# The mLSTM heads' normalisation: column sums on TensorE and a small inverse root, or squares added first, two products of ones, and an inverse root over whole rows

## The chip, the cores and the metric

The kernel runs on one core of a Trainium2 chip. The metric is the device time of one execution in microseconds (us). The kernel before took 1197.71 us, the median of three runs (1197.57 to 1198.04).

The engines are named as in the profile: PE is TensorE's matmul, PEld its weight load, DVE is VectorE, ACT is ScalarE, POOL is GpSimd, and SP is SyncE, which issues most of the loads. "L175" is line 175 of the kernel.

## The reference

The reference is a two-layer streaming encoder over 512 positions and a width of 1024. Layer 0 mixes with an mLSTM (4 heads of 192 columns) and an attention to 256 memory tokens, layer 1 with a chunked band attention and the same kind of memory attention; each layer has a gated MLP with a short convolution behind it. The change touches only what stands behind the mLSTM's weighted sums:

```python
h = num / jnp.maximum(jnp.abs(den), jnp.exp(-m_t))[..., None]
...
hm = hm * lax.rsqrt(jnp.mean(hm * hm, axis=-1, keepdims=True) + EPS)
hm = hm.reshape(bsz, seq, A_WIDTH) * a_head_g[a].astype(jnp.float32)
mix_out = (hm * jax.nn.sigmoid(o.astype(jnp.float32))).astype(x.dtype)
```

`num` is a head's weighted sum of values, `den` the same sum of ones, `m_t` a running maximum of the gates. The kernel never divides by the denominator. With z = max(den^2, exp(-2 m_t)), the normalised row is num / sqrt(mean(num^2) + EPS * z), so that one factor for each position is enough: the inverse root of mean(num^2) + EPS * z.

## The kernel before, in words

Everything is held transposed: columns of the model on the 128 partitions, the 512 positions along the free dimension. A product of full precision is three products of split operands (`mm3`, lines 175 to 177: high by high, high by low, low by high); `split` (L136, L137) makes the two halves, the high one as a copy on ScalarE and the low one as a subtraction on VectorE. Weights come by SP in tiles of 128 columns, go through `split`, and are used by `project`.

`gate_rows` computes the rows of the gates (4 partitions, one for each head, by 512 positions): `ar`, `mr` and running sums, with a maximum of `mr` at L1086. Lines 1096 and 1097 transpose `ar` and `mr` in blocks of 128 positions, so that positions come onto the partitions; L1099 takes exp(-2 mr) there as `floor2` (128 x 4 x 4). It runs beside the value columns and the q, k and o tiles of the first head pair, which call it as filler.

`mlstm_head(h)` has three parts. First the weighted scores in four blocks of keys and the products with the values (L1151 to L1191), which give two banks: `nums[0]` has 128 columns of the head, and `nums[1]` has the other 64 on one half of the partitions (`rs`) and, on the other half, the denominator, 64 times the same row, since the value tiles hold ones there. Then the squares (L1195, ScalarE) and the products of the sums with the o gate (L1197, VectorE). Then the normalisation:

- For each block T of 128 positions, two products (L1202, L1203) with the squares as the stationary operand and two columns of constants (`mcf`) as the moving one. They give, with positions on the partitions, the sum of squares and the mean of the 64 squared denominators.
- L1207 to L1210: the maximum with `floor2`, the factor EPS, the mean, and an inverse root by an integer trick and three Newton steps (`rsqrt`, L219 to L228), all on 128 x 4.
- `diagonal` (L230 to L244) splits the 128 x 4 result and puts each half on four diagonals of 128 x 128; `spread` (L246 to L251) multiplies them with ones (L250), so that the factor of each position stands on all partitions, in a `psc` bank.
- L1216 multiplies the gated sums with it, and `split` puts the result into `mixes`, which the output projection (`OutProjection`) reads.

A head is a generator; `yield n` tells `weave` how much filler to put there. In the first three heads the filler is the projections of the q, k and o tiles and the memory queries, in the fourth head the products of the output projection whose inputs are there already. Between heads 1 and 2 and between heads 2 and 3 stands a memory attention. The parts (0, 4, 5) and (1, 4, 5) of the output projection need heads 2 and 3 and come last. Then `OutProjection.finish` starts the next norm; its `logarithms()` (L255) loads the table set of ScalarE that has both logarithm and exponential.

In this part of the kernel a scheduler orders each engine's instructions, by what is ready and by the order of the program; `pin` keeps an instruction behind the one that its engine was given before. Buffers: three PSUM banks `mm`, three `sc`, two `tr`; eight rows `t`, two rows `bias` (the band attention of layer 1 uses them later).

`Norm.finish` (L272 to L289), used by the norms of whole rows, has a form of its own: `split` of the summed squares, two products of ones (L280), logarithm, exponential and square on ScalarE (L282, L284, L285), and two VectorE operations for one Newton step (L287, L289).

Of the kernel before, what the change touches and what calls it, by code (L numbers as in the profile page):

```python
# [9 lines left out]
F32 = mybir.dt.float32  # L10
F32R = mybir.dt.float32r
I32 = mybir.dt.int32
AF = mybir.ActivationFunctionType
ALU = mybir.AluOpType
AX = mybir.AxisListType

P = 128
D = 1024
S = 512
KT = D // P  # L20
TT = S // P
MEM = 256
AW = 768
AH = 4
DH = AW // AH
BH = 12
HD = 64
# [3 lines left out]
EPS = 1e-6  # L31
# [24 lines left out]
def trunk(  # L56
# [30 lines left out]
    def sb(tag, shape, dtype=F32):  # L87
        count[0] += 1
        return pool.tile(shape, dtype, tag=tag, name=f"{tag}{count[0]}", bufs=bufs[tag])

    def ps(tag):
        count[0] += 1
        return psum.tile([P, S], F32, tag=tag, name=f"p{tag}{count[0]}", bufs=pbufs[tag])

    def small(n=4):
        return sb("s", [P, 32])[:, :n]
# [21 lines left out]
            V.tensor_copy(sel[q], ident[q, 32 * s : 32 * s + AH].unsqueeze(2).to_broadcast([AH, AH, P]))  # L118
    eps = cpool.tile([P, 1], F32, name="eps")
    V.memset(eps, EPS)  # L120

    mcf = cpool.tile([P, 3, 2], F32, name="mcf")
    V.memset(mcf, 0.0)
    V.memset(mcf[:, 0, 0:1], 1.0)
    V.memset(mcf[:HD, 1, 0:1], 1.0)
    V.memset(mcf[HD:, 1, 1:2], 1.0 / HD)
    V.memset(mcf[:HD, 2, 1:2], 1.0 / HD)
    V.memset(mcf[HD:, 2, 0:1], 1.0)


    HEADS = (slice(0, HD), slice(HD, P))

# [2 lines left out]
    def split(hi, lo, src, on_act=True, pinned=False):  # L135
        high = A.copy(hi, src) if on_act else V.tensor_copy(hi, src)  # L136
        low = V.tensor_tensor(out=lo, in0=src, in1=f(hi), op=ALU.subtract)  # L137
        if pinned:
            pin(high)
            pin(low)  # L140
# [78 lines left out]
    def rsqrt(y, v):  # L219
        n = v.shape[-1]  # L220
        yi = y.bitcast(I32)
        V.tensor_scalar(yi, v.bitcast(I32), 1, None, op0=ALU.logical_shift_right)
        V.tensor_scalar(yi, yi, -1, 0x5F3759DF, op0=ALU.mult, op1=ALU.add)
        t = small(n)
        for _ in range(3):
            V.tensor_mul(t, y, y)
            V.scalar_tensor_tensor(t, t, -0.5, v, op0=ALU.mult, op1=ALU.mult)
            V.scalar_tensor_tensor(y, t, 1.5, y, op0=ALU.add, op1=ALU.mult)  # L228

    def diagonal(c):  # L230

        cs = [sb("s", [P, 32], F32R)[:, :TT] for _ in range(2)]
        split(*cs, c, on_act=False)
        dgs = []
        for c in cs:
            dg = sb("t", [P, S], F32R)
            V.tensor_tensor(
                out=dg.rearrange("p (a b) -> p a b", a=TT),
                in0=ident.unsqueeze(1).to_broadcast([P, TT, P]),
                in1=f(c).unsqueeze(2).to_broadcast([P, TT, P]),  # L240
                op=ALU.mult,
            )
            dgs.append(dg)
        return dgs  # L244

    def spread(dgs, tag):  # L246

        o = ps(tag)
        for i, dg in enumerate(dgs):
            nc.tensor.matmul(o, onesr, dg, start=i == 0, stop=i == 1)  # L250
        return o  # L251

    def logarithms():

        pin(A.preload_act_table_set("natural_log_exp_and_others"))  # L255
# [762 lines left out]
    e, u, c, r = (cpool.tile([P, TT, AH], F32, name=f"gate{i}") for i in range(4))  # L1018
    tot = cpool.tile([AH, 16], F32, name="tot")
    acol = cpool.tile([P, TT, AH], F32, name="acol")  # L1020
    floor2 = cpool.tile([P, TT, AH], F32, name="floor2")
    RO = [0, 512, 896, 1152, 1280]

    rp = []
# [1 line left out]
    def gate_rows():  # L1026

        V.tensor_copy(ic, gt[:, :, :AH])
        V.scalar_tensor_tensor(e, fg, -1.0, fg, op0=ALU.mult, op1=ALU.min)
        A.activation(e, e, AF.Exp)  # L1030
        V.tensor_scalar(u, e, 1.0, None, op0=ALU.add)
        A.activation(lf, u, AF.Ln)
        V.scalar_tensor_tensor(c, u, -1.0, e, op0=ALU.add, op1=ALU.subtract)
        V.reciprocal(r, u)
        yield
        pin(V.tensor_mul(c, c, r))
        V.tensor_tensor(out=lf, in0=lf, in1=c, op=ALU.subtract)
        V.scalar_tensor_tensor(lf, fg, 0.0, lf, op0=ALU.min, op1=ALU.subtract)
        yield
        yield  # L1040
        lfp, icp = ps("tr"), ps("tr")
        for T in range(TT):
            nc.tensor.transpose(lfp[:AH, T * P : (T + 1) * P], lf[:, T, :], ident)
            nc.tensor.transpose(icp[:AH, T * P : (T + 1) * P], ic[:, T, :], ident)
        yield
        lfr, br, ar, mr = (sb("t", [P, S])[:AH, :] for _ in range(4))
        rr = [sb("t", [P, S]) for _ in range(2)]
        rp.extend(sb("u", [P, S], F32R) for _ in range(2))
        for t in rp:
            G.memset(f(t), 0.0)  # L1050
        pin(V.tensor_copy(lfr, lfp[:AH, :]))
        yield
        for T in range(TT):
            sl = slice(T * P, (T + 1) * P)
            pin(V.tensor_tensor_scan(br[:, sl], ones[:AH, :], lfr[:, sl], 0.0, ALU.mult, ALU.add))
        yield
        pin(V.tensor_tensor(out=ar, in0=icp[:AH, :], in1=br, op=ALU.subtract))
        yield
        carry = 0.0
        for T in range(TT):  # L1060
            sl = slice(T * P, (T + 1) * P)
            pin(V.tensor_tensor_scan(mr[:, sl], ar[:, sl], ar[:, sl], carry, ALU.max, ALU.max))
            if T < TT - 1:
                e_ = (T + 1) * P - 1
                V.tensor_tensor(out=tot[:, T : T + 1], in0=mr[:, e_ : e_ + 1], in1=br[:, e_ : e_ + 1], op=ALU.add)
                carry = tot[:, T : T + 1]
            yield
        for s in range(TT):
            off = None
            for T in range(s, TT):  # L1070
                sl = slice(T * P, (T + 1) * P)
                dst = rr[s // 2][64 * (s % 2) : 64 * (s % 2) + AH, sl]
                if T == s:
                    pin(V.tensor_scalar(dst, mr[:, sl], -1.0, None, op0=ALU.mult))
                else:
                    end = br[:, T * P - 1 : T * P]
                    if off is None:
                        off = end
                    else:
                        k = 4 + 4 * s + T - s  # L1080
                        V.tensor_tensor(out=tot[:, k : k + 1], in0=off, in1=end, op=ALU.add)
                        off = tot[:, k : k + 1]
                    V.tensor_scalar(dst, mr[:, sl], -1.0, off, op0=ALU.mult, op1=ALU.add)
            yield
        pin(V.tensor_tensor(out=mr, in0=mr, in1=br, op=ALU.add))
        V.tensor_scalar(mr, mr, -40.0, None, op0=ALU.max)  # L1086
        yield
        for s in range(TT):
            q, t = 64 * (s % 2), rp[s // 2]
            src, hi = rr[s // 2][q : q + AH, s * P :], t[q : q + AH, s * P :]  # L1090
            pin(V.tensor_copy(hi, src))
            V.tensor_tensor(out=t[q + 32 : q + 32 + AH, s * P :], in0=src, in1=f(hi), op=ALU.subtract)
            yield
        tp = ps("tr")
        for T in range(TT):
            nc.tensor.transpose(tp[:, T * AH : (T + 1) * AH], ar[:, T * P : (T + 1) * P], ident[:AH, :AH])
            nc.tensor.transpose(tp[:, 16 + T * AH : 16 + (T + 1) * AH], mr[:, T * P : (T + 1) * P], ident[:AH, :AH])
        pin(V.tensor_copy(acol, tp[:, :16].rearrange("p (t h) -> p t h", t=TT)))
        A.activation(floor2, tp[:, 16:32].rearrange("p (t h) -> p t h", t=TT), AF.Exp, scale=-2.0)  # L1099

    mixes = [None] * KT

# [41 lines left out]
    def mlstm_head(h):  # L1144
# [48 lines left out]
        for o, j, r in ((nums[0], full, slice(0, P)), (nums[1], sh, rs)):  # L1193
            sq = sb("t", [P, S])
            A.activation(sq, o, AF.Square)  # L1195
            sqs.append(sq)
            V.tensor_tensor(out=og[j][r, :], in0=o[r, :], in1=og[j][r, :], op=ALU.mult)  # L1197
        yield
        st = ps("sc")
        for T in range(TT):  # L1200
            sl = slice(T * P, (T + 1) * P)
            nc.tensor.matmul(st[:, 2 * T : 2 * T + 2], sqs[0][:, sl], mcf[:, 0, :], start=True, stop=False)  # L1202
            nc.tensor.matmul(st[:, 2 * T : 2 * T + 2], sqs[1][:, sl], mcf[:, 1 + odd, :], start=False, stop=True)  # L1203
            yield 0.581
        st = st[:, : 2 * TT].rearrange("p (t c) -> p t c", c=2)
        z, fc = small(), small()
        V.tensor_tensor(out=z, in0=st[:, :, 1], in1=floor2[:, :, h], op=ALU.max)  # L1207
        V.tensor_scalar(z, z, EPS, 1e-35, op0=ALU.mult, op1=ALU.max)
        V.scalar_tensor_tensor(z, st[:, :, 0], 1.0 / DH, z, op0=ALU.mult, op1=ALU.add)
        rsqrt(fc, z)  # L1210
        dg = diagonal(fc)
        yield 2.673
        fb = spread(dg, "sc")
        yield
        for j, r in ((full, slice(0, P)), (sh, rs)):
            V.tensor_tensor(out=og[j][r, :], in0=fb[r, :], in1=og[j][r, :], op=ALU.mult)  # L1216
# [308 lines left out]
```

## Time and profile before

| what | value |
| --- | --- |
| median of three runs | 1197.71 us |
| span of the profiled execution (first to last instruction) | 1197.4 us |
| instructions in it | 18206 |
| mLSTM heads' column sums (L1202, L1203) | from 125.2 to 247 us |
| ACT table loads of L1112, L582, L255, L1157 | 6, 3, 3, 2 |
| one table load | 1283 ns |
| mean granted TensorE clock | 0.999 |

The page gives the profiled execution's span and no other time for it. Busy times are sums over instructions; a busy matmul time overlaps with its neighbours', since matmuls are pipelined, so that distances between starts are the better measure. In a timeline each line has the start, the duration, engine, line, operation, output <- input, shape, the count and, in brackets, the idle time before it with what ended it. A line of the windows view has the stretch, its length, then busy time and count for PE, PEld, DVE, ACT and POOL, the granted clock, the share of the DMA engines and GB/s. A line of a group has count, busy time, mean duration, and the idle time before. A line of waits has who waited for whom, the total, how often, and the longest.

### The profile page before, as it was taken

Reading aid. Unit: us, or ns where it says so; the run is one execution under the profiler, and the core shown is the slowest. Engines: PE = TensorE matmul, PEld = TensorE weight load, DVE = VectorE, ACT = ScalarE, POOL = GpSimd, SP = SyncE. Lnnn points to the kernel's source line nnn. Section 1 sums busy time; section 2 is a strip of 40 time slices with the busy share of each in tenths; the row PEclk is TensorE's granted clock in tenths of the full one; section 3 lists DMA queues with packets and bytes.
Section 4 is the critical chain, followed back from the end, with each engine's and each line's share of the span. In section 5 each row is a group of like instructions: output and inputs, shape, how many; then the busy total and the mean of one; then the engine's idle time right before and its main releaser. Section 6 shows DMA issues by size and latency. Waiting matters only on the chain.

```text
span 1197.4 us, 18206 instructions
## 1 busy us (share of the span) xinstructions
PE 1186.5 (99%) x6735; PEld 1039.1 (87%) x6735; DVE 967.3 (81%) x1772; ACT 718.4 (60%) x1290; POOL 123.3 (10%) x206
## 2 busy tenths in 40 slices
PE   9999999999999999999999999999999999999997
PEld 8988888888889989999888888888889988999986
DVE  6778688878978888888698888997897888888855
ACT  5646577655655555555575667776565655555545
POOL 1200101000021111111021000001001011011100
PEclk9999999999999999999999999999999999999999
DMA  8634111454266666665563223146336466665551
GB/s 283 212 92 123 54 54 57 134 152 133 88 157 162 153 162 155 151 144 129 152 189 120 89 71 99 55 130 201 116 89 150 110 138 141 141 141 136 121 158 71
DMA packets 199131, 155.97 MB, mean 130 GB/s; under 512 B 7976, under 2 KB 179458, under 8 KB 199042
## 3 DMA queue, kind: packets, MB, share of 16 engines
q1 hardware_dynamic: 183906, 119.74, 34.2%
q0 software_dynamic: 14560, 34.02, 13.7%
q8 instruction: 53, 0.87, 0.3%
q10 hardware_dynamic: 576, 1.05, 0.2%
q14 instruction: 36, 0.29, 0.1%
HBM read 126.27 MB, written 32.44 MB: 133 GB/s over the span
## 4 chain that ended last, share of the span: by engine, by line
PE 93%; DMA 2%; ACT 2%; DVE 2%; issue 0%; SPq 0%; ACTq 0%; DVEq 0%
PE pmm L175 15%; PE pmm L176 15%; PE pmm L177 15%; PE ptr L175 6%; PE ptr L177 6%; PE ptr L176 6%; PE pmm L791 6%; PE psc L177 5%; PE psc L175 5%; PE psc L176 5%; PE pmm L790 3%; PE psc L525 2%; DMA wr<-in_mem_w_kv_dram 2%; PE ptr L1352 1%; PE ptr L1373 1%; PE ptr L1374 1%
## 5 line engine op out<-in xcount | busy, mean ns | idle before, releaser
L175 PE MATMUL pmm<-u,wh 128*128 128x512 f32 (+1 forms) x872 | 309.1, 355 | 0.3 <-ACT u L136 0.2
L176 PE MATMUL pmm<-u,wh 128*128 128x512 f32 (+1 forms) x872 | 306.3, 351 | 0.0
L177 PE MATMUL pmm<-u,wl 128*128 128x512 f32 (+1 forms) x872 | 306.3, 352 | 0.0
L137 DVE TENSOR_TENSOR wl<-wr,wh 128x1024 fp32r<-128x1024 f32 (+3 forms) x172 | 199.8, 1163 | 55.1 <-ACT wh L136 53.1
L136 ACT CAST wh<-wr 128x1024 fp32r<-128x1024 f32 (+3 forms) x172 | 172.1, 1002 | 99.8 <-PE pmm L176 45.2
L177 PEld LDWEIGHTS pmm<-u,wl 128*128 128x128 f32 x872 | 164.5, 189 | 20.9
L175 PEld LDWEIGHTS pmm<-u,wh 128*128 128x128 f32 x872 | 164.5, 189 | 18.7 <-ACT u L136 1.1
L176 PEld LDWEIGHTS pmm<-u,wh 128*128 128x128 f32 x872 | 164.7, 189 | 18.3 <-DVE u L137 0.5
L175 PE MATMUL ptr<-u,wh 128*128 128x512 f32 x272 | 106.7, 392 | 0.0
L177 PE MATMUL ptr<-u,wl 128*128 128x512 f32 x272 | 106.1, 390 | 0.0
L176 PE MATMUL ptr<-u,wh 128*128 128x512 f32 x272 | 105.9, 389 | 0.0
L759 POOL DMA_DIRECT2D xspill<-t x64 | 55.5, 867 | 462.5 <-ACT t L758 457.1
L136 ACT CAST u<-pt 128x512 fp32r<-128x512 f32 x102 | 62.8, 618 | 47.2 <-DVE pt L881 47.1
L137 DVE TENSOR_TENSOR u<-pt,u 128x512 fp32r<-128x512 f32 x102 | 69.9, 689 | 11.2 <-ACT u L136 8.5
L175 PE MATMUL psc<-u,wh 128*128 128x256 f32 (+1 forms) x232 | 76.1, 328 | 0.0
L177 PE MATMUL psc<-u,wl 128*128 128x256 f32 (+1 forms) x232 | 75.9, 327 | 0.0
L176 PE MATMUL psc<-u,wh 128*128 128x256 f32 (+1 forms) x232 | 75.9, 327 | 0.0
L791 PE MATMUL pmm<-u,u 128*128 128x512 f32 x192 | 69.6, 397 | 0.0
L943 ACT ACTIVATE t<-t 128x512 f32<-128x512 f32 x34 | 21.5, 632 | 79.4 <-DVE t L666 79.4
L827 DVE TENSOR_TENSOR t<-t,pmm 128x256 f32<-128x256 f32 x72 | 30.2, 420 | 45.0 <-ACT t L825 45.0
L758 ACT COPY t<-ptr 128x512 f32<-128x512 f32 x64 | 37.4, 584 | 42.8 <-PE ptr L177 42.8
L666 DVE SCALAR_TENSOR_TENSOR t<-t,cols,t 128x511 f32<-128x511 f32 x80 | 59.6, 746 | 3.7 <-ACT t L673 3.7
(305 smaller groups left out, 2671.5 us busy)
## 6 DMA issues: line engine op xcount, KB each, us to landing
wr<-in_ffn_w_up_dram SPq DMA_DIRECT2D x54, 512.0 KB, 4.5
wr<-in_ffn_w_down_dram SPq DMA_DIRECT2D x38, 512.0 KB, 4.1
pt<-in_ffn_w_up_dram SPq DMA_DIRECT2D x34, 512.0 KB, 6.0
xspill<-t POOLq DMA_DIRECT2D x64, 256.0 KB, 5.2
wr<-in_a_w_in_dram SPq DMA_DIRECT2D x20, 512.0 KB, 3.7
xspill<-u POOLq DMA_DIRECT2D x32, 256.0 KB, 2.7
u<-xspill SPq DMA_DIRECT2D x32, 256.0 KB, 5.1
wr<-in_w_kv_dram SPq DMA_DIRECT2D x12, 512.0 KB, 3.8
```

What stands on the lines that cost most here:

```text
L136: high = A.copy(hi, src) if on_act else V.tensor_copy(hi, src)
L137: low = V.tensor_tensor(out=lo, in0=src, in1=f(hi), op=ALU.subtract)
L175: nc.tensor.matmul(o, lh, rh, start=first, stop=False, skip_group_check=more)
L176: nc.tensor.matmul(o, lh, rl, start=False, stop=False, skip_group_check=more)
L177: nc.tensor.matmul(o, ll, rh, start=False, stop=last, skip_group_check=more)
L525: nc.tensor.matmul(o, a, b, start=first and i == 0, stop=i == 1)
L666: V.scalar_tensor_tensor(acc[:, n:], src[:, : S - n], self.fw[:, c * FT + j : c * FT + j + 1], acc[:, n:], op0=ALU.mult, op1=ALU.add,)
L758: A.copy(t, o)
L759: G.dma_start(xspill[j], t, accum_op=ALU.add)
L790: nc.tensor.matmul(r[:, :H], w[1][:, k], p[i - 1][:, :H], start=False, stop=False, skip_group_check=True)
L791: nc.tensor.matmul(r, w[0][:, k], p[i - 1], start=False, stop=k == n - 1, skip_group_check=True)
L827: V.tensor_tensor(out=o, in0=o, in1=r[:, H:], op=ALU.add)
```

## The change

The constants `mcf` go. `floor2` becomes four rows in DRAM: in `gate_rows` the rows `mr` are bounded at -29, an exponential with factor -2 is taken, EPS * 192 / 64 is multiplied in and the result is kept above 1e-19; POOL stores the rows, and four POOL transfers read them back, each row onto 64 partitions, into two `bias` rows (`floors`, one for each head pair). The transposes of `mr` go.

In the head, the half of the second squares that holds the denominators is scaled by EPS * 192 / 64 and bounded by `floors`; both squares are added, and the sum is split. The table set is loaded by `logarithms()`; after filler, two products of ones (`spread`) sum over partitions and put the sum, which is 192 times mean(num^2) + EPS * z, onto all partitions. Logarithm, exponential and square follow on ScalarE, and one Newton step on VectorE. The product with the gated sums is as before, but its factor is a row `t` and no PSUM bank.

```diff
-    mcf = cpool.tile([P, 3, 2], F32, name="mcf")
-    V.memset(mcf, 0.0)
...
-    floor2 = cpool.tile([P, TT, AH], F32, name="floor2")
+    floor2 = dram.tile([AH, S], F32, name="floor2")
+    floors = []
...
-        V.tensor_scalar(mr, mr, -40.0, None, op0=ALU.max)
+        V.tensor_scalar(mr, mr, -29.0, None, op0=ALU.max)
+        A.activation(mr, mr, AF.Exp, scale=-2.0)
+        V.tensor_scalar(mr, mr, EPS * DH / HD, 1e-19, op0=ALU.mult, op1=ALU.max)
+        G.dma_start(floor2, mr)
+        for hp in range(2):
+            floors.append(sb("bias", [P, S]))
+            for odd, half in enumerate(reversed(HEADS)):
+                row = floor2[2 * hp + odd]
+                src = bass.AP(tensor=row.tensor, offset=row.offset, ap=[[0, HD], [1, S]])
+                G.dma_start(floors[hp][half, :], src)
...
-            nc.tensor.transpose(tp[:, 16 + T * AH : 16 + (T + 1) * AH], mr[:, T * P : (T + 1) * P], ident[:AH, :AH])
...
-        A.activation(floor2, tp[:, 16:32].rearrange("p (t h) -> p t h", t=TT), AF.Exp, scale=-2.0)
...
+        dr = HEADS[1 - odd]
+        V.scalar_tensor_tensor(
+            sqs[1][dr, :], sqs[1][dr, :], EPS * DH / HD, floors[hp][dr, :], op0=ALU.mult, op1=ALU.max
+        )
+        V.tensor_add(sqs[0], sqs[0], sqs[1])
+        halves_ = [sb("t", [P, S], F32R) for _ in range(2)]
+        split(*halves_, sqs[0])
         yield
-        st = ps("sc")
-        for T in range(TT):
-            sl = slice(T * P, (T + 1) * P)
-            nc.tensor.matmul(st[:, 2 * T : 2 * T + 2], sqs[0][:, sl], mcf[:, 0, :], start=True, stop=False)
-            nc.tensor.matmul(st[:, 2 * T : 2 * T + 2], sqs[1][:, sl], mcf[:, 1 + odd, :], start=False, stop=True)
-            yield 0.581
-        st = st[:, : 2 * TT].rearrange("p (t c) -> p t c", c=2)
-        z, fc = small(), small()
-        V.tensor_tensor(out=z, in0=st[:, :, 1], in1=floor2[:, :, h], op=ALU.max)
-        V.tensor_scalar(z, z, EPS, 1e-35, op0=ALU.mult, op1=ALU.max)
-        V.scalar_tensor_tensor(z, st[:, :, 0], 1.0 / DH, z, op0=ALU.mult, op1=ALU.add)
-        rsqrt(fc, z)
-        dg = diagonal(fc)
-        yield 2.673
-        fb = spread(dg, "sc")
+        logarithms()
+        yield 3.4
+        o = spread(halves_, "sc")
+        t, fb = sb("t", [P, S]), sb("t", [P, S])
+        A.activation(t, o, AF.Ln, scale=1.0 / DH)
+        A.activation(fb, t, AF.Exp, scale=-0.5)
+        A.activation(t, fb, AF.Square)
+        yield 2
+        V.scalar_tensor_tensor(t, t, -0.5 / DH, o, op0=ALU.mult, op1=ALU.mult)
+        V.scalar_tensor_tensor(fb, t, 1.5, fb, op0=ALU.add, op1=ALU.mult)
         yield
```

More of the change, by code (lines that the diff above doesn't have):

```diff
@@ L120, in trunk @@
     V.memset(eps, EPS)
-    mcf = cpool.tile([P, 3, 2], F32, name="mcf")
-    V.memset(mcf, 0.0)
[L124 to L128, printed above, removed]
     HEADS = (slice(0, HD), slice(HD, P))
```

## The prediction, made before the changed kernel was run

> **What bounds the kernel now.** I read the page first, from its head line through the busy row to the chain of work that ended last.
>
> ```profile
> span 1197.4 us, 18206 instructions
> PE 1186.5 (99%) x6735; PEld 1039.1 (87%) x6735; DVE 967.3 (81%) x1772; ACT 718.4 (60%) x1290; POOL 123.3 (10%) x206
> ...
> PE 93%; DMA 2%; ACT 2%; DVE 2%; issue 0%; SPq 0%; ACTq 0%; DVEq 0%
> ```
>
> TensorE is busy all the time and 93% of the chain is its own. So an edit is worth what it takes out of the TensorE queue, less the time in which that queue then stands still. Next I read the windows view: the gate rows (61 to 107 us), the end of each of the four heads (123:137, 149:162, 205:218, 243:257) and the memory attention behind head 1 (166:189). Its columns are PE, PEld, DVE, ACT and POOL busy, each with its count.
>
> ```profile
> 61.00:107.00 46.00, 46.00 (x226) 39.46 (x226) 36.42 (x69) 24.98 (x35) 0.00 (x0) 1.00 0.37 103
> 123.00:137.00 14.00, 14.00 (x72) 11.80 (x72) 10.83 (x28) 7.47 (x10) 0.14 (x1) 1.00 0.28 77
> 149.00:162.00 13.00, 13.00 (x71) 11.16 (x71) 11.15 (x28) 7.31 (x10) 0.00 (x0) 1.00 0.18 48
> 166.00:189.00 23.00, 23.00 (x113) 18.85 (x111) 18.09 (x34) 22.33 (x42) 0.00 (x0) 1.00 0.21 56
> 205.00:218.00 13.00, 13.00 (x65) 10.55 (x64) 10.93 (x29) 4.69 (x8) 0.00 (x0) 1.00 0.17 55
> 243.00:257.00 14.00, 13.84 (x70) 11.26 (x69) 10.77 (x28) 6.11 (x8) 0.00 (x0) 1.00 0.25 72
> ```
>
> At each head's end TensorE is full, at granted clock 1.00, while ACT is busy for about half of it (7.47 of 14, 7.31 of 13, 4.69 of 13, 6.11 of 14). Two facts will matter: 166:189 is full on ACT too (22.33 of 23), and 243:257 is the one stretch where TensorE is not quite full.
>
> **The change part by part.** *Removed from TensorE: the column sums, 8 products a head with two columns each.* "Busy" of pipelined matmuls overlaps, so I count from start to start, in the timeline of head 0.
>
> ```profile
> 125.15 0.40 PE L177 MATMUL pmm<-u,wl 128*128 128x512 f32 x1
> 125.38 0.28 PE L1202 MATMUL psc<-mcf,t 128*128 128x2 f32 x2
> 125.52 0.36 PE L1203 MATMUL psc<-mcf,t 128*128 128x2 f32 x2
> 125.74 0.47 PE L175 MATMUL pmm<-u,wh 128*128 128x512 f32 x1
> 126.06 0.39 PE L176 MATMUL pmm<-u,wh 128*128 128x512 f32 x1
> ...
> 126.52 0.28 PE L1202 MATMUL psc<-mcf,t 128*128 128x2 f32 x2
> ...
> 127.33 0.47 PE L175 MATMUL pmm<-u,wh 128*128 128x512 f32 x1
> 127.64 0.39 PE L176 MATMUL pmm<-u,wh 128*128 128x512 f32 x1
> ```
>
> A large product's successor starts 0.23 us after it (125.15 to 125.38). A group of L1202 and L1203 takes 0.36 (125.38 to 125.74), and the product behind it needs 0.32 instead of 0.23: 0.45 us. Two groups in a row take 0.81 + 0.08 = 0.89 (126.52 to 127.33, then 0.31). Four groups make 1.78 to 1.80 us a head: **5.4 us for heads 0 to 2 and 1.8 for head 3.**
>
> *Also removed:* four of the eight small transposes behind the gate rows, 0.06 us each by their starts, together **0.24 us.**
>
> ```profile
> 98.51 0.20 PE L1097 MATMUL ptr<-ident,t 4*128 4x4 f32 x1
> 98.57 0.20 PE L1096 MATMUL ptr<-ident,t 4*128 4x4 f32 x1
> ```
>
> The two products of ones (L250) stay two. The memsets of mcf go at the start, where the chain of work runs through DMA (its 2%): 0.
>
> *VectorE.* Sixteen operations on 128x4 and the two diagonals go from each head:
>
> ```profile
> L237 DVE TENSOR_TENSOR t<-ident,s 128x512 fp32r<-128x512 f32 x8 | 5.1, 685 | 0.0
> ...
> L226 DVE TENSOR_TENSOR s<-s 128x4 f32<-128x4 f32 x12 | 1.9, 162 | 0.4
> ```
>
> 16 x 0.162 + 2 x 0.685 = 4.0 us. Bound, sum, low half and two Newton steps come instead, five passes over 512 columns at about 0.69 (L270, L137, L287 and L289 below): 3.4 us. VectorE is not worse off.
>
> *ScalarE.* Each head gains a copy 0.62, a logarithm 0.69, an exponential 0.63, a square 0.63 and a load of the table set: 2.6 + 1.28.
>
> ```profile
> L582 ACT ACT_TABLE_LOAD x3 | 3.8, 1283 | 0.1
> ```
>
> The next exponential then finds its set in place, unless a Tanh or Silu came between, so the loads about balance, or one is added. That is 3.9 us against 5.7 to 8.3 us free at each head's end: no cost there. The gate rows get an exponential earlier, among the Silu of the q and k tiles, hence about two more loads (2.6 us); ACT has 21 us free between 61 and 107. Cost 0; if the cover fails, at most those 2.6 us, because a late weight cast delays products.
>
> *Queues.* POOL gets one store and four broadcast loads. The store must land before the loads go, and whatever POOL has next is queued behind that wait. The nearest row is a POOL transfer that waits for another through DRAM, at most 6.2 us:
>
> ```profile
> POOL rep L1260 <- DMA rep<-in_b_rel_row_dram: 69.2, 12, 6.2
> ```
>
> POOL does nothing from 61 to 107 (x0 above) and the first bound is read at about 124. Cost 0; the other end is those 6.2 us once, if the first mask of head 0 (L1159, near 109) stood behind the wait. SP issues nothing new.
>
> *The chain of a head.* The new sequence from the sum on (split, two products of ones, logarithm, exponential, square, two steps) is in the trace already, in Norm.finish:
>
> ```profile
> 281.04 0.68 DVE L270 TENSOR_TENSOR rb<-rb,t 128x512 f32<-128x512 f32 x1
> ...
> 281.76 0.62 ACT L136 CAST t<-rb 128x512 fp32r<-128x512 f32 x1 [0.75 <-DVE rb L270]
> ...
> 282.41 0.69 DVE L137 TENSOR_TENSOR t<-rb,t 128x512 fp32r<-128x512 f32 x1
> ...
> 284.22 0.69 ACT L282 ACTIVATE t<-psc,eps 128x512 f32<-128x512 f32 x1 [1.84 <-PE psc L280]
> ...
> 284.81 1.04 ACT L136 CAST wh<-wr 128x1024 fp32r<-128x1024 f32 x1
> ...
> 285.74 0.63 ACT L284 ACTIVATE t<-t 128x512 f32<-128x512 f32 x1
> ...
> 286.41 0.63 ACT L285 ACTIVATE t<-t 128x512 f32<-128x512 f32 x1
> ...
> 287.07 0.69 DVE L287 SCALAR_TENSOR_TENSOR t<-t,rb 128x512 f32<-128x512 f32 x1
> ...
> 287.80 0.69 DVE L289 SCALAR_TENSOR_TENSOR rb<-t,t 128x512 f32<-128x512 f32 x1
> ```
>
> From the end of the sum (281.72) to the finished row (288.49) are 6.77 us, with a weight cast slipped in between logarithm and exponential; without it about 6.0. For heads 0 to 2 the chain's length is hidden: nothing behind it is wanted soon, and projections of q, k and o tiles fill TensorE. For **head 3** it is not hidden, because the last products of the output projection need its result and there is no other work:
>
> ```profile
> 245.01 0.69 DVE L1197 TENSOR_TENSOR u<-ptr,u 64x512 f32<-64x512 f32 x1
> ...
> 252.35 1.42 DVE L1216 TENSOR_TENSOR u<-psc,u 128x512 f32<-128x512 f32 x2 [0.80 <-PE psc L250]
> ...
> 252.81 1.28 ACT L255 ACT_TABLE_LOAD   x1
> ...
> 254.10 1.26 ACT L136 CAST u<-u 128x512 fp32r<-128x512 f32 x2
> ...
> 254.87 0.39 PE L177 MATMUL ptr<-u,wl 128*128 128x512 f32 x1
> ...
> 255.42 0.97 PE L175 MATMUL pmm<-u,wh 128*128 128x512 f32 x3 [0.16 <-ACT u L136]
> ```
>
> Now TensorE runs out at 255.10 (254.87 + 0.23) and goes on at 255.42: chain and filler end almost together. Without its column sums the filler ends at 255.10 - 1.80 = 253.30. The new chain in the same coordinates: the second product with the gate ends at 245.70, bound 246.4, sum 247.1, row 247.1 + 6.77 = 253.9, two products with the row 1.42, the second cast 0.65: **256.0**, where it was 255.42. So head 3 gives back all of its 1.8 us and 0.6 more. From both sides: 255.2 with no cast slipped in; 258.2 if the set load of the next norm (1.28, now at 252.81) and a weight split of 0.96 also fall into it. I take 256.0, the nearest row's own length.
>
> Norm.finish leaves 1.84 us of ACT between copy and logarithm, so a load of 1.28 fits into it. [...]
>
> **Sum:** 5.4 + 0.24 - 0.6 = 5.0 us. The profiled span is 1197.4 us (the page gives that execution no other time); the median of the runs is 1197.71, 0.3 above. 1197.4 - 5.0 + 0.3 = **1192.7 us.**
>
> **The rivals.** *All of it (1190.3).* If the chain of head 3 keeps level with the shortened filler (done by 253.6, with smaller gaps than Norm.finish shows), the 1.8 us stay: 7.2 + 0.24 = 7.4. For it: the set is already in place, so the next norm's load may leave the way. Against: the chain would have to be 2.4 us shorter than its own copy in the trace.
>
> *A wait takes the removed work's place (1196.3).* The result of the products of ones now holds its psc bank through logarithm, exponential, square and a Newton step, and six t buffers are in use. If the next scores or the next softmax wait for these at the ends of heads 1 and 2 as well, they too give back their 1.8: 5.0 - 3.6 = 1.4 us left. Against it: the products of 14 projections stand by as filler, and TensorE takes it whenever a head waits.
>
> *Slower: ScalarE becomes the bound in the memory attention (1203).* If the passes of heads 1 and 2 come so late that they land in the two memory attentions behind them, they meet a full ACT (22.33 of 23 us), and each microsecond there delays the softmax and the weight casts, thus TensorE. With a Silu or Tanh between preload and logarithm another load is due. Price: 2 x (2.6 + 1.28 + 1.28) = 10.3 us, against the 5.0: 5.3 slower. It decides from the point where more than 5.0 us of this lands there. For it: ACT serves its queue in order, and the preload stands behind the Silu ahead of it. Against: 5.7 and 8.3 us are free at the ends of heads 1 and 2, directly before.
>
> **How the numbers follow.** Forecast 0.52, all of it 0.20, wait instead 0.16, slower 0.12. The forecast's own range is 1191.5 to 1195 (the ends 255.2 and 258.2). A measurement here tells about 0.2%, 2.4 us, from no change. Faster: forecast, all of it and a little of the third, 0.74; same: nearly all of the third, 0.15; slower: 0.11. The range leaves out the lower half of "all of it" and the slower rival: 1189.9 to 1197.6.
>
> **What would show it.** Right: no products of 128x2 on TensorE, 123:137 to 205:218 without idle TensorE and each head's stretch 1.8 us shorter, and at the end of head 3 a wait of TensorE of 2 to 3 us for ACT's cast or VectorE's low half. Wrong: no wait there (all of it); waits of TensorE for psc or t at the starts of scores (third); over 23 us of ACT work in the first memory attention, or three or more set loads between a head's preload and its exponential (slower).

## The result, and the profile after

The changed kernel takes **1202.86 us** (median; 1201.45 to 1204.26) against 1197.71 (1197.57 to 1198.71): ratio 1.0040, 95% interval 1.0029 to 1.0051. It is slower by 0.4%, where 1192.7 was forecast. The profiled execution took 1201.45 us, the quickest of these runs. First the page of the changed kernel: its head, the busy row and the chain of work.

```profile
span 1199.7 us, 18046 instructions
...
PE 1183.6 (99%) x6667; PEld 1032.5 (86%) x6667; DVE 966.6 (81%) x1715; ACT 741.8 (62%) x1316; POOL 126.1 (11%) x211
...
PE 92%; DVE 4%; ACT 3%; issue 1%; POOL 0%; DVEq 0%; ACTq 0%; POOLq 0%
```

TensorE is busy for 2.9 us less, as the change meant it, but the chain now goes through VectorE (4%) and ScalarE (3%), which had 2% each. The busy time of ScalarE rose by 23 us. The windows of before, read again in the changed kernel, show where:

```profile
123.00:137.00 14.00, 13.96 (x60) 10.90 (x59) 9.47 (x13) 11.39 (x15) 0.61 (x1) 1.00 0.27 75
149.00:162.00 13.00, 12.68 (x61) 10.25 (x60) 11.56 (x16) 9.58 (x15) 0.00 (x0) 1.00 0.30 83
166.00:189.00 23.00, 21.05 (x94) 16.72 (x93) 16.44 (x32) 21.06 (x38) 1.17 (x1) 0.93 0.23 65
205.00:218.00 13.00, 12.64 (x56) 10.02 (x55) 9.08 (x14) 9.43 (x14) 0.00 (x0) 1.00 0.06 16
243.00:257.00 14.00, 11.62 (x53) 8.72 (x51) 9.11 (x13) 9.68 (x13) 0.00 (x0) 1.00 0.25 72
```

The ends of heads 0 to 2 are still nearly full on TensorE. The first memory attention (166:189) was full and now lacks 1.95 us, at a granted clock of 0.93 on the mean; head 3's end lacks 2.4. The list of TensorE's waits from 110 to 262 us (who waited for whom, total, times, longest) was two waits of 0.2 us before. Now:

```profile
PE pmm L166 <- ACT u L127: 2.1, 1, 2.1
PE ptr L599 <- DVE pt L128: 1.5, 2, 0.8
PE psc L1154 <- ACT t L573: 0.9, 1, 0.9
PE psc L241 <- ACT t L127: 0.7, 2, 0.4
PE psc L166 <- ACT t L1156: 0.5, 1, 0.5
PE ptr L166 <- DVE u L1196: 0.3, 1, 0.3
PE ptr L585 <- DVE t L576: 0.2, 1, 0.2
...
```

The first row and the 0.3 us in front of the ptr product L166 are head 3's end. L1154, L585 and one L599 lie in the first memory attention, the other L599 and the psc product L166 in the second. L241 is the start of the products of ones in heads 1 and 2, which wait for the high half. Here is TensorE in the first attention:

```profile
180.14 0.39 PE L168 MATMUL pmm<-u,wl 128*128 128x512 f32 x1
181.44 0.44 PE L1154 MATMUL psc<-u,sel 128*128 128x384 f32 x1 [0.91 <-ACT t L573]
182.12 0.63 PE L585 MATMUL ptr<-ident,t 128*128 128x128 f32 x4 [0.24 <-DVE t L576]
183.55 3.50 PE L599 MATMUL ptr<-pt,u 128*128 128x512 f32 x8 [0.80 <-DVE pt L128]
186.85 0.61 PE L166 MATMUL pmm<-u,wh 128*128 128x512 f32 x1
```

The value products (L599) stand in the queue directly behind the last transposes (L585) and wait out the split of what these wrote; the next products of projections stand behind them in the queue. Before, four transposes at 180.49 were followed by 15 products and then by the first four value products at 184.35, without a wait. And the eight value products take 3.30 us from start to next start, 0.41 each. The windows of one microsecond say why (the third number from the right is the granted clock):

```profile
183.00:184.00 1.00, 0.45 (x2) 0.41 (x3) 1.00 (x2) 0.97 (x2) 0.00 (x0) 0.95 0.00 0
184.00:185.00 1.00, 1.00 (x4) 0.73 (x3) 1.00 (x3) 0.00 (x0) 0.00 (x0) 0.50 0.00 0
...
187.00:188.00 1.00, 1.00 (x5) 0.77 (x4) 0.81 (x1) 0.99 (x2) 0.97 (x1) 0.85 0.00 0
```

From 183.9 to 187.3, 3.4 us, TensorE has half its clock (0.50). What that costs can be read against n1_step3 (below), which differs from the changed kernel only in head 3. Its profiled execution has the same waits here and kept its clock (its eight products take 2.45 us, those of e1_no_sets, at a clock of 1.00, take 2.46):

```profile
184.10 2.45 PE L599 MATMUL ptr<-pt,u 128*128 128x512 f32 x8 [0.80 <-DVE pt L128]
186.39 0.40 PE L166 MATMUL pmm<-u,wh 128*128 128x512 f32 x1
```

From start to next start they take 2.29 us there. With the products behind them, the half clock costs 1.2 us at this place, beside the 1.95 us of idleness; at the squares of head 2 the two executions are 0.8 us apart. What TensorE waited for at 181.44 is in ScalarE's timeline:

```profile
174.55 1.28 ACT L1111 ACT_TABLE_LOAD   x1
175.85 0.63 ACT L1111 ACTIVATE t<-t 128x512 f32<-128x512 f32 x1
176.50 1.28 ACT L573 ACT_TABLE_LOAD   x1
177.79 0.48 ACT L573 ACTIVATE t<-psc,s 128x256 f32<-128x256 f32 x1
...
178.26 1.28 ACT L497 ACTIVATE u<-t 64x512 fp32r<-64x512 f32 x2
...
180.82 0.48 ACT L573 ACTIVATE t<-psc,s 128x256 f32<-128x256 f32 x1
```

TensorE's wait ends with the pass of 180.82, the last of the softmax (L573). A Silu (L1111) with a set load on each side, 3.2 us, cuts this softmax, and so do four passes for the queries that come of the Silu's result (L497 and L500, 178.26 to 180.81). Before, all passes of the softmax were through at 177.8, and the Silu and these four came behind them. In the groups of ScalarE there are 30 set loads where before had 20. Silu (L1111) has nine in place of six, the preload (L246) seven in place of three, and the heads' logarithm and exponential (L1209, L1210) have two of their own:

```profile
L1111 ACT ACT_TABLE_LOAD x9 | 11.5, 1283 | 8.3 <-DVE t L1110 8.1
L246 ACT ACT_TABLE_LOAD x7 | 9.0, 1283 | 0.1
L573 ACT ACT_TABLE_LOAD x3 | 3.8, 1283 | 0.1
...
L1209 ACT ACT_TABLE_LOAD x1 | 1.3, 1283 | 0.0
L1210 ACT ACT_TABLE_LOAD x1 | 1.3, 1283 | 0.0
```

At head 3's end the forecast's picture stands:

```profile
244.37 0.69 DVE L1196 TENSOR_TENSOR u<-ptr,u 128x512 f32<-128x512 f32 x1 [2.40 <-ACT t L1194]
...
245.69 0.69 DVE L1196 TENSOR_TENSOR u<-ptr,u 64x512 f32<-64x512 f32 x1
...
250.66 0.60 ACT L1209 ACTIVATE t<-psc 128x512 f32<-128x512 f32 x1
...
254.51 0.39 PE L168 MATMUL ptr<-u,wl 128*128 128x512 f32 x1
254.55 1.41 DVE L1217 TENSOR_TENSOR u<-t,u 128x512 f32<-128x512 f32 x2
...
256.97 0.96 PE L166 MATMUL pmm<-u,wh 128*128 128x512 f32 x3 [2.07 <-ACT u L127]
```

The last filler product makes room for a next one at 254.74 (254.51 + 0.23), and the chain ends at 256.97. The profile counts 2.07 us of this as a wait; 2 to 3 was forecast.

One thing on the baseline: in every run of both kernels that has a span, the time is about 1.7 us above it, so the profiled execution of before (span 1197.4) was itself some 1.4 us slower than its median. Its first product of ones, early in the kernel, starts at 30.63 us, in the changed kernel at 29.09; the part up to there varies from run to run. So I count stages from that product on. The table has, for each kernel, its median time and these stages in its profiled execution, all as the start in the timeline less the start of that first product: the squares of head 2, those of head 3, and the products of ones of the next norm.

| kernel | time | squares 2 | squares 3 | next norm |
| --- | --- | --- | --- | --- |
| before | 1197.71 | 174.86 | 212.43 | 252.93 |
| after | 1202.86 | 176.33 | 214.65 | 256.39 |
| g0_rows_only | 1198.16 | 175.20 | 212.78 | 253.28 |
| g5_head0_new | 1197.76 | 173.84 | 211.42 | 251.94 |
| g1_head3_old | 1199.98 | 176.71 | 214.99 | 255.44 |
| e1_no_sets | 1200.13 | 176.10 | 212.37 | 255.17 |
| w1_weave | 1199.09 | 172.69 | 210.98 | 254.01 |
| r1_retuned | 1199.34 | 172.54 | 210.82 | 254.09 |
| d1_awake | 1198.67 | 172.60 | 210.91 | 252.65 |
| r2_step3_retuned | 1195.79 | 172.62 | 210.93 | 250.45 |
| n1_step3 | 1199.34 | 175.53 | 213.81 | 253.36 |
| n2_steps_weave | 1194.51 | 172.82 | 209.47 | 248.98 |
| n3_steps_only | 1194.20 | 174.14 | 210.75 | 250.29 |
| n5_order | 1193.55 | 172.33 | 208.98 | 248.47 |

Each row of stages is one execution, and not always one near its kernel's median: that of n3_steps_only took 1196.72 us, the slowest of its six.

### The profile page after: what moved, and what is told of

Same layout as the page of the kernel before. It is cut to its first block, busy times and chain, and to the rows that moved or that the text cites. A ratio compares the mean times of both kernels' runs of the same rounds, so it can differ in the third digit from the quotient of the medians.

```text
span 1199.7 us, 18046 instructions
## 1 busy us (share of the span) xinstructions
PE 1183.6 (99%) x6667; PEld 1032.5 (86%) x6667; DVE 966.6 (81%) x1715; ACT 741.8 (62%) x1316; POOL 126.1 (11%) x211
## 4 chain that ended last, share of the span: by engine, by line
PE 92%; DVE 4%; ACT 3%; issue 1%; POOL 0%; DVEq 0%; ACTq 0%; POOLq 0%
PE pmm L166 15%; PE pmm L167 15%; PE pmm L168 15%; PE pmm L782 6%; PE ptr L167 6%; PE ptr L168 6%; PE ptr L166 5%; PE psc L168 5%; PE psc L166 5%; PE psc L167 5%; PE pmm L781 3%; PE psc L516 2%; PE ptr L1353 1%; PE ptr L1374 1%; PE ptr L1375 1%
## 5 line engine op out<-in xcount | busy, mean ns | idle before, releaser
L166 PE MATMUL pmm<-u,wh 128*128 128x512 f32 (+1 forms) x872 | 308.6, 354 | 2.2 <-ACT u L127 2.1
L166 PEld LDWEIGHTS pmm<-u,wh 128*128 128x128 f32 x872 | 164.6, 189 | 21.2 <-ACT u L127 3.0
L166 PE MATMUL ptr<-u,wh 128*128 128x512 f32 x272 | 106.5, 392 | 0.3 <-DVE u L1196 0.3
L166 PE MATMUL psc<-u,wh 128*128 128x256 f32 (+1 forms) x232 | 76.1, 328 | 0.0
## 6 DMA issues: line engine op xcount, KB each, us to landing
xspill<-t POOLq DMA_DIRECT2D x64, 256.0 KB, 5.2
xspill<-u POOLq DMA_DIRECT2D x32, 256.0 KB, 3.2
u<-xspill SPq DMA_DIRECT2D x32, 256.0 KB, 4.9
```

Of the source, the lines that this page charges most:

```text
L166: nc.tensor.matmul(o, lh, rh, start=first, stop=False, skip_group_check=more)
```

## The experiments

My theory (T1): the loss lies in the first memory attention, where ScalarE's and TensorE's queues came out in another order, so that TensorE stands still and its clock falls. T2: it is head 3's exposed chain. Rivals: the gate rows, the set loads of the heads, the passes themselves. Ratios are to the kernel before, with 95% intervals.

**g0_rows_only.** Only the gate rows of the change; the heads' column sums, inverse root and diagonals stand again under the first branch.

```diff
+            nc.tensor.transpose(tp[:, 16 + T * AH : 16 + (T + 1) * AH], mr[:, T * P : (T + 1) * P], ident[:AH, :AH])
...
+        A.activation(floor2s, tp[:, 16:32].rearrange("p (t h) -> p t h", t=TT), AF.Identity, scale=1.0 / (EPS * DH / HD))
...
+        if h in (0, 1, 2, 3):
...
+            V.tensor_tensor(out=z, in0=st[:, :, 1], in1=floor2s[:, :, h], op=ALU.max)
...
+        else:
```

> All four heads normalise by the form of before (column sums, integer trick, diagonals); of the change only the gate rows are kept: exponential, factor, store and four loads of the rows, which nothing reads but the four small transposes put back. T1 (the loss lies in the memory attention, where TensorE stands still and its clock is then halved) and T2 (head 3's exposed chain) both say that this costs nothing: 1197 to 1199 us, clock 0.999, TensorE full from 168 to 187. The rival that the gate rows' loads, their two added set loads or POOL's wait delay the heads' start says 1200 us or more.

1198.16 us, ratio 1.0004 (0.9995 to 1.0013), waits of TensorE as before (two of 0.2). The rows, their store and loads and two set loads cost nothing that can be measured; the rival falls.

**g5_head0_new.** The same with head 0 in the new form: `h in (1, 2, 3)`.

> Only head 0 in the new form, heads 1 to 3 as before, gate rows as changed (1198.2 with all four as before). It prices the removal itself where filler covers the chain, and 15 products stand before the value products of the first memory attention as before. The sum's term of 1.8 us a head: 1196.4. If the three added set loads of this head (25 in place of 22) cost TensorE 1.28 us each, 1198 to 1200.

1197.76 us, 0.9999 (0.9990 to 1.0008). No new wait of TensorE; the added set loads are hidden. At all three stages it is 1.34 to 1.36 us ahead of g0_rows_only. So by this one pair of executions a head's column sums are worth 1.35 us, not 1.8; of it 0.4 is left in the medians, which differ by less than they can tell. The expected 1196.4 was not reached, and 1198 or more did not come either.

**g1_head3_old.** Heads 0 to 2 new, head 3 as before: `h in (3,)`.

> Heads 0 to 2 as changed, head 3 in the form of before (its floor comes from transposes as in before). By T2 alone (head 3's chain of 12.1 us with 2.3 us of idle TensorE is the loss) the time falls from 1202.9 to about 1198. By T1 alone (memory attention) it stays at 1202 to 1203, for head 3 only gives back its own 1.8 us against 2.3 us of idleness, thus -0.5. Both together: about 1202.

1199.98 us, 1.0019 (1.0010 to 1.0029): 2.9 us better than the change and still slower than before: neither T2's 1198 nor T1's 1202, so both hold a part. Up to head 3 nothing has changed (214.99 against 214.65), and the eight value products take 3.69 us here, where the changed kernel's take 3.50 at its low clock. At the next norm it is 0.95 us ahead in the profiled executions; the medians have 1.9 us more than that. About 1.4 of it can be the clock behind head 3's wait (d1_awake): the changed kernel's profiled execution kept its clock there (1.00 from 257 to 261).

**e1_no_sets.** The heads without set switches (other values).

```diff
-        logarithms()
...
-        A.activation(t, o, AF.Ln, scale=1.0 / DH)
-        A.activation(fb, t, AF.Exp, scale=-0.5)
+        A.activation(t, o, AF.Identity, scale=1.0 / DH)
+        A.activation(fb, t, AF.Identity, scale=-0.5)
```

> The changed kernel with logarithm and exponential of the heads replaced by passes of the same size that need no other table set, and without the preload in the heads: other values, six set loads less (24 in place of 30), TensorE's order in the first memory attention the same. T1a (the heads' own set loads, 6 x 1.28 = 7.7 us of ScalarE, make the softmax late): 1198 to 1199. T1b (the set loads between softmax and Silu inside the memory attention, three pairs here too, and TensorE's order, in which the value products follow the last transposes at once): 1201 to 1202, idle TensorE at 180 to 184 as before.

1200.13 us, 1.0019 (1.0010 to 1.0027), between the two expectations. The first attention's waits are the same as in the change (0.91, 0.24 and 0.80 us), and squares 2 come nearly as late (176.10 against 176.33): its idleness does not come from the heads' set loads. From squares 2 to squares 3 it takes 36.27 us instead of 38.32, and TensorE has no wait in the second attention. The clock in the first attention is another:

```profile
184.07 2.46 PE L599 MATMUL ptr<-pt,u 128*128 128x512 f32 x8 [0.80 <-DVE pt L128]
```

2.46 us where the changed kernel's profile has 3.50: in this execution the clock stayed at 1.00 here (184 to 187). Behind head 3's wait of 2.07 us it fell instead: products start 0.43 us apart from 256.97 to 257.82, and 0.23 later. Its eleven runs go from 1198.7 (mean clock 0.998) to 1201.96 (0.995).

**w1_weave.** One number of the changed kernel.

```diff
-    weave(memory_attention(memq[0], memkv, 0, mixes), fill, 1.463, 4)
+    weave(memory_attention(memq[0], memkv, 0, mixes), fill, 1.8, 4)
```

> The changed kernel with one number changed: filler per step of the first memory attention 1.8 in place of 1.463. All up to there is the same; inside it the last softmax is no longer cut by a Silu (two set loads less) and three products stand between the last transposes and the value products, four more before the second half. T1: the idleness and the halved clock of 180 to 187 go, 1199 to 1200. T2 (head 3) or the heads' own set loads: no change, 1202 to 1203.

1199.09 us, 1.0011 (1.0002 to 1.0020): 3.8 us better. Squares 2 move by 3.64 us. Of this 1.95 us are the idleness and 0.8 the clock (n1_step3); the rest, 0.9, is traced only in part: two groups of four value products take 1.92 us here, the row of eight 2.29. The number changes two things at once, which are not separated: no Silu cuts the last softmax, and three products stand behind the last transposes:

```profile
182.81 0.60 PE L585 MATMUL ptr<-ident,t 128*128 128x128 f32 x4
183.16 0.48 PE L166 MATMUL pmm<-u,wh 128*128 128x512 f32 x1
...
183.95 1.08 PE L599 MATMUL ptr<-pt,u 128*128 128x512 f32 x4
```

**r1_retuned.** All operations of the change, three other filler numbers.

```diff
-        yield 3.4
+        yield 2.5
...
-        yield 2
+        yield 1
...
-    weave(mlstm_head(0), fill, 1.4)
+    weave(mlstm_head(0), fill, 1.6)
```

> All of the change, other filler numbers only: 2.5 and 1 in the head's end in place of 3.4 and 2, and 1.6 per step of head 0 in place of 1.4. The order that comes of it has 25 set loads (30 as changed, 20 before), none between the last two softmax pairs, and 19 products between the last transposes and the value products of the first memory attention. T1 (order and set loads, not the operations themselves, make the first attention's loss): its idleness and halved clock go, 1197.5 to 1199; head 3's wait of about 2 us and the second attention's 1.7 us stay. Rival (the added passes themselves are too much for ScalarE there): 1201 or more.

1199.34 us, 1.0011 (1.0002 to 1.0020), 3.5 us better than the change. The first attention is full again:

```profile
168.00:190.00 22.00, 22.00 (x106) 18.05 (x105) 20.94 (x37) 21.35 (x41) 0.80 (x2) 1.00 0.28 85
```

ScalarE is as busy there (21.35 of 22) as before the change (21.36): it was the order and not the amount of work. The stretch from squares 2 to 3 stays at 38.28.

**b1_old3_weave.** g1_head3_old with 1.8 for 1.463.

> Head 3 in the form of before (worth 2.9 us alone) and filler 1.8 in the first memory attention (worth 3.8 alone), heads 0 to 2 as changed. If the two losses are separate and add: 1202.9 - 2.9 - 3.8 = 1196.2, faster than before by some 1.5. If both runs only spared the same halved clock (one period of about 1.7 us counted twice): about 1198, no better than before. Idle TensorE left: the second memory attention (1.7 us) and the starts of spread (0.7).

1198.77 us, 1.0005 (0.9996 to 1.0014): in the medians the two do not add. Up to the next norm its profile has what they promise (251.70, or 4.7 us ahead of the change; w1_weave's 3.67 at squares 3 and g1_head3_old's 0.95 make 4.6), but from there to the end it takes 0.6 to 1.2 us longer than the other kernels of the table. I found no wait there that explains it; that stays open.

**n1_step3.** The changed kernel, head 3 without square and Newton step: `if h < 3:` before L1211, L1213 and L1214.

> The changed kernel, but head 3 leaves out its square and its Newton step (the row is the exponential itself): 0.63 + 2 x 0.69 = 2.0 us less in the chain, nothing else. T2 (the chain's length is what TensorE waits for at head 3's end): the wait of 2.07 us shrinks to about 0.1, the clock no longer falls there, 1202.9 - 2.0 to 3.2 = 1199.7 to 1200.9. Rival (the weight cast and the set load in front of the last casts set the end): wait 1.5 or more, 1202 or more.

1199.34 us, 1.0009 (1.0000 to 1.0018): 3.5 better for 2.0 us of chain. The wait shrank from 2.07 to 0.3 us. T2 holds at its place. In the profiled executions 2.19 of the 3.03 us at the next norm arise behind squares 3; the other 0.84 is the clock of the first attention, which this execution happened to keep. The clock behind head 3's wait, which the changed kernel's profiled execution kept, would add to the gain in others (1.4 us by d1_awake, an estimate).

**r2_step3_retuned.** r1_retuned and n1_step3 together.

> As the one with other filler numbers, and head 3 alone without square and Newton step. Both losses taken away at their places; if they add (3.5 us for head 3's step by its own run), 1194.5 to 1195.5; left is the second memory attention's idleness (1.7 us). If they share one halved clock, 1196 to 1197.

1195.79 us, 0.9982 (0.9973 to 0.9991). It is level with r1_retuned up to squares 3 (210.93 and 210.82) and 3.64 us ahead at the next norm. The two losses add: 3.5 us from r1_retuned here, as n1_step3 had 3.5 from the changed kernel.

**d1_awake.** What goes beside the idleness? r1_retuned with nine products that nothing reads, at head 3's end.

```diff
-    run(chain(fill, outp.part(0, 4, 5), outp.part(1, 4, 5)))
+    run(fill)
+    idle = ps("sc")
+    for _ in range(9):
+        nc.tensor.matmul(idle, onesr, mixes[6][0], start=True, stop=True)
+    run(chain(outp.part(0, 4, 5), outp.part(1, 4, 5)))
```

> The version with other filler numbers (1199.34 us, 1.0011 of before; head 3 with its square and Newton step), and nine products of ones, which nothing reads, in TensorE's queue just where it stands still for 2.07 us at head 3's end: 9 x 0.23 = 2.05 us. If the halved clock behind such a wait is a cost of its own (products there start 0.43 us apart in place of 0.23, for about 3 us): the added products save it, clock 0.998 or more, 1197.7 to 1198.3 and runs closer together. If the idleness alone is the loss and the clock a by-product: no gain, 1199.3 to 1199.6.

1198.67 us, 1.0009 (1.0000 to 1.0019): between the two expectations, and 0.7 us off r1_retuned is little beside the spread of the runs (1197.91 to 1200.78), which did not come closer together. The clock says more: over eleven runs each, the mean granted clock of a run is 0.996 to 0.998 in r1_retuned and 0.998 to 0.999 here. And in the two profiled executions work that nobody needs comes with a next norm 1.44 us earlier (252.65 and 254.09). First TensorE in r1_retuned:

```profile
253.47 0.96 PE L166 MATMUL pmm<-u,wh 128*128 128x512 f32 x3 [2.07 <-ACT u L127]
...
256.13 0.63 PE L167 MATMUL pmm<-u,wh 128*128 128x512 f32 x1
256.56 0.63 PE L168 MATMUL pmm<-u,wl 128*128 128x512 f32 x1
```

and then in d1_awake:

```profile
251.57 2.26 PE L1250 MATMUL psc<-u,onesr 128*128 128x512 f32 x9
253.79 0.96 PE L166 MATMUL pmm<-u,wh 128*128 128x512 f32 x3
...
255.77 0.40 PE L168 MATMUL pmm<-u,wl 128*128 128x512 f32 x1
256.00 0.39 PE L167 MATMUL pmm<-u,wh 128*128 128x512 f32 x1
```

The useful products resume as late after the filler as before (2.22 us, the added products in between), but start 0.23 us apart instead of 0.43; from 254 to 258 the granted clock is 1.00 here and 0.63 on the mean in r1_retuned. So the lower clock is a cost of its own, 1.4 us between these two executions.

**n2_steps_weave and n3_steps_only.** No square and Newton step in any head; n2 with 1.8 for 1.463 as well.

```diff
-        A.activation(t, fb, AF.Square)
         yield 2
-        V.scalar_tensor_tensor(t, t, -0.5 / DH, o, op0=ALU.mult, op1=ALU.mult)
-        V.scalar_tensor_tensor(fb, t, 1.5, fb, op0=ALU.add, op1=ALU.mult)
```

> The changed kernel with filler 1.8 in the first memory attention and without square and Newton step in any head: ScalarE 0.63 and VectorE 1.38 us less a head, head 3's chain 2.0 us shorter. If the loss is idle TensorE behind ScalarE and VectorE, as T1 and T2 say: 1199.1 (filler alone) - 2.0 to 3.0 = 1196 to 1197, and faster than before. Rival (something that no wait of TensorE shows): 1198 or more.

> No square and no Newton step in any head, filler as in the changed kernel. If the steps' absence is what made the version with both 1194.5 us: 1194 to 1195.5. If the filler number made it: near 1199.3 less some 1 us for the free ScalarE, 1197.5 to 1198.5.

1194.51 (0.9969, 0.9958 to 0.9981) and 1194.20 (0.9967, 0.9955 to 0.9979). n2 is some 2 us faster than expected, n3 as expected if the filler number is not needed. In both the list of TensorE's waits has none in either attention, and 0.3 us where head 3's 2.07 were. From squares 2 to 3 n2 takes 36.65 us where w1_weave takes 38.29, so the second attention is relieved as in e1_no_sets. The number of set loads does not decide that: n2 has 26, and r1_retuned, which waits there, 25. Less work and the other order that comes with it are not separated.

**n5_order.** As n3, with the filler numbers 2.5, 0.5 and 1.6 (24 set loads).

> No square and no Newton step in any head, filler numbers 2.5 and 0.5 and 1.6: 24 set loads in place of 26, 15 products before the value products of the first memory attention. The set loads of the heads are hidden work by then, so 1194 to 1194.6, no better than with filler 1.8; if each set load still costs TensorE its 1.28 us, 1192.

1193.55 us, 0.9964 (0.9952 to 0.9977), the best of all and faster than both kernels; it leaves out the Newton step, so its inverse root is that of logarithm and exponential alone. Its windows of the two attentions:

```profile
168.00:190.00 22.00, 22.00 (x106) 18.35 (x105) 19.28 (x33) 19.16 (x32) 0.84 (x3) 1.00 0.20 61
228.00:260.00 32.00, 31.30 (x148) 25.02 (x147) 24.01 (x37) 21.69 (x34) 4.85 (x9) 1.00 0.45 133
```

The two set loads less than n3 go with 0.65 us between the medians, which is too little to tell.

## Why the prediction was wrong, step by step

- *Removed from TensorE, 1.8 us a head:* right in kind, too large: 1.35 by g5_head0_new. Over four heads that is 1.8 us less gain than the sum had. Where the other 0.45 of a head stays was not traced.
- *Gate rows and queues, 0:* right (g0_rows_only).
- *Head 3 gives back its 1.8 and 0.6 more:* right as to the chain. From the end of the second product with the gate to the resumption 10.3 us were forecast (245.70 to 256.0) and 10.6 measured (246.38 to 256.97). It left out the clock, which such a wait can cost: another 1.4 us where it fell (r1_retuned, 0.63 from 254 to 258, against d1_awake, 1.00). The changed kernel's profiled execution doesn't have that loss, r1_retuned's has; the changed kernel's median lies 1.4 us above that execution, and the other runs' mean clocks are 0.995 to 0.997 against its 0.998, which fits it.
- *"That is 3.9 us against 5.7 to 8.3 us free at each head's end: no cost there":* **this is the step that failed.** It is true at the heads' ends themselves, where TensorE lacks 0.04 to 0.36 us. But I counted ScalarE's time in the window in which the program has the passes, and did not ask what the work does to the order behind it. *"The loads about balance, or one is added"* (for each head; with two for the gate rows, six at most) became ten more loads; e1_no_sets, whose heads need no other set, has six fewer. In the first memory attention a Silu and four passes behind it moved ahead of the last softmax pass, and the value products moved up to the last transposes. In place of 0 this cost 3.65 us at squares 2: 1.95 us idle, 0.8 of clock, and slower starts. w1_weave and r1_retuned take all of that away without removing one operation of the change. In the second attention another 2 us or so went, and which of work and order took them stays open. The switch of set at 176.50 took its load and hardly more: the load, 1.28 us long, starts 0.02 us behind the Silu, and the exponential 1.29 us behind the load's start.
- *VectorE is not worse off:* held (966.6 us busy against 967.3). The third rival's waits at the starts of scores came, 0.91 us (L1154, head 2) and 0.47 (L166, head 3), but inside the attentions and behind exponentials (L573, L1156), not for the bank of the products of ones. TensorE also waits 0.32 and 0.36 us in front of L241, in heads 1 and 2.
- *The slower rival (1203)* named the right places and was given 0.12. That its time fits 1202.86 is luck: its price, 10.3 us of passes and loads that TensorE waits out one by one, is not what was lost, and its mechanism, a full ScalarE in the memory attentions, is right for neither. In the first ScalarE was less busy than before (20.04 of 22 us in 168:190 against 21.36), and r1_retuned is full on TensorE at 21.35. In the second it was less busy too (the fourth of the busy times, before and then the changed kernel):

```profile
218.00:240.00 22.00, 21.82 (x118) 18.05 (x116) 17.80 (x37) 17.71 (x41) 1.95 (x4) 1.00 0.52 166
218.00:240.00 22.00, 20.60 (x107) 16.07 (x105) 18.85 (x38) 16.02 (x38) 1.16 (x4) 1.00 0.66 208
```

TensorE waits there 0.74 us for a split on VectorE in front of the value products (L599) and 0.47 for an exponential of the next scores. The stretch from squares 2 to 3 takes 38.3 us, 36.3 without set switches and 36.7 without the steps.
- *"TensorE takes it whenever a head waits",* said of the filler against the third rival, fails in the attentions: the queue is fixed ahead, and the products behind a waiting one did not start before it. In the changed kernel's first attention the value products wait 0.80 us and start at 183.55, and the projections behind them start at 186.85.
- *Two small things in the sum:* 1197.4 is a span and not a time, but what comes of it is the median less 5.0 all the same. And 255.2 at head 3's end gives 1191.9 as the lower end of the forecast's own range, not 1191.5.

The sum in the profiled executions, from the first product of ones to the next norm: 4 x 1.35 + 0.24 removed is -5.6; first attention +3.65; second +2.1 with head 2's wait at L241 (38.32 less 37.57, and head 2's 1.35); head 1's wait at L241 +0.3; head 3's waits +2.4. That is +2.8, against +3.46 measured (256.39 less 252.93); the other 0.7 us are not assigned. With the clock behind head 3 in the median runs, +1.4, the measured 3.46 comes near the 5.15 us between the medians. What tipped the scheduler to the worse order in the first attention was not traced: with head 0 alone in the new form there is no wait there, with heads 0 to 2 there is.

## What to carry to other kernels

Where an engine's queue is laid out ahead, a change of an operation is also a change of order: look at what stands behind each product that must wait, and retune the filler numbers before judging the operation (3.5 to 3.8 us here, of 5.15 that the change lost). Passes that need another table set are to be counted with the passes of other sets that the scheduler can put between them (here a Silu with a load on each side, 3.2 us, inside a softmax), not by the free time of the engine. And a short wait of TensorE is to be priced with the clock that follows it (1.2 and 1.4 us here, beside waits of 2 us).

## What the runs showed of the hardware

Waits of 2 us in all cost 1.2 us (the changed kernel against n1_step3, in the first attention) and 1.4 us (r1_retuned against d1_awake) more through the clock where it fell. In the changed kernel it fell to 0.50 for 3.4 us (183.9 to 187.3) after 1.95 us of idleness in three pieces, the longest 0.91 us. In r1_retuned, after waits of 2.07 and 0.21 us, it was 0.63 on the mean from 254 to 258, and products started 0.43 us apart instead of 0.23. The same waits lost the clock in one execution and kept it in another: the same eight products, behind the same queue, took 3.50 us in the changed kernel and 2.45 in n1_step3, and behind head 3's waits of 2.07 and 0.20 us the changed kernel's clock stayed at 1.00 (257 to 261). What decides between the two was not shown.
